# Differential attention scores from products of 64 rows in the two row halves of the TensorE array

## The chip, the cores and the metric

The kernel runs on one core of a Trainium2 chip. The metric is the device time in microseconds of one execution, as the median of several runs. Engines are named as in the profile: PE is the matrix engine (TensorE), PEld its weight loads, DVE the vector engine, ACT the scalar engine, POOL GpSimd, SP the queue that issues most DMAs.

## The reference

One layer of a streaming encoder on two inputs: a prompt of 1024 tokens (8 tiles of 128) and a running stream of 64 new tokens (the ninth tile, i = 8) with 128 cached keys and values. A norm and one input projection give two branches: retention (8 heads of 64) and differential attention (4 heads). Each differential head has two components of 64 columns with a softmax each, and values of 128 columns:

```
logits = einsum('bqhcd,bkhcd->bhcqk', q, k) * 64**-0.5      # c: two components
p = softmax(where(mask, logits, NEG_BIG))                   # block-causal, chunks of 64
w = p[:, :, 0] - lam * p[:, :, 1]
o = einsum('bhqk,bkhe->bqhe', w, v)
```

Both branches are normalised, gated and sent through an output projection; a residual add and a final norm close the layer. Everything is float32.

## The kernel before

The work is eight projection groups, alternately two retention heads (R, four times) and one differential head (D, four times). Group g makes, for each of 9 token tiles, a product `z` of the tile with 512 columns of the input weights, over 8 slices of the contraction; an output projection `zo` follows at the end. Projections and scores use fp32r, which keeps fewer bits; so each operand is split into a high part (rounded to fp32r) and a low part (what is left), and a projection is high·high + low·high + high·low.

After a projection, a chain of stages works on the tile: `diff_post` for D, `ret_post` for R. They are Python generators. Each `yield` gives a due time, in nanoseconds of PE work by the program's own count `clk.t`, and the buffers that the next stage needs. `pump`, called after each slice of a projection, issues the stages that are due and whose buffers are free. So the order on PE is fixed when the program is built, and PE works in that order: a late input stops everything behind it. The due times that matter here are D_QK and D_SPLIT (2600 each: from the projection to the transpose, from the transpose to the scores), D_SC (1600, between the two halves of the scores), D_SOFT and D_SOFT2 (3500 and 6500, from the scores to the transpose of the weights, for tiles with one and with two segments). `share` is new in the change; before, `mm` counts every product at its full columns.

A D tile goes like this, by the lines of the profile:
- L298 to L311: copy q and k, rotary on 16 columns.
- L323 (recorded at L68): two transposes into the PSUM tile `T`: 64 partitions of component 0, then 64 of component 1, for q and for k.
- L336 to L342, the split. Product operands of 128 rows are stacked: for component 0 `qs` is [high; low] of q, `khh` [high; high] of k and `kll` [low; low] of k, so that a product with `khh` and one with `kll` sum all four terms. It takes six ACT copies and six DVE differences on 64 partitions, alternating, component by component. `khh` and `kll` hold all keys of the head so far.
- L359 and L360 (recorded at L63): the scores `s`, per component and per segment of up to 512 keys, two products each. Tile i sees 128(i+1) keys: one segment up to i = 3, two from i = 4 to 7; tile 8 has one of 192. Each segment of a component has its own PSUM bank, tag `m`, of which there are five; transposes and the retention scores use the same tag.
- L363 (DVE): the negative maximum `nm`; L366 the smaller of two segments; L368 (ACT): the exponential `p` with its sum. These follow a component's products at once; component 1 comes a stage later.
- L376 to L381 (DVE): weights, p0 + factor·p1. L391 to L412: their transposes `wt` and the products `o` with v. L421: norm and gate, `mx`, transposed again as `mt`.

At tile 8 the cached keys come by DMA, already doubled to both halves, and are split by one ACT and one POOL instruction (L332, L333).

Of the kernel before, what the change touches and what calls it, by code (L numbers as in the profile page):

```python
# [20 lines left out]
SEQ = 1024  # L21
NS = 64
PAST = 128
# [3 lines left out]
NEG_BIG = -1e30  # L27
# [4 lines left out]
# PE time (ns) that the weave keeps between a stage of a tile's chain and the next one  # L32
D_QK, D_SPLIT, D_SC, D_SOFT, D_SOFT2, D_WT, D_WT2, D_NORM = 2600, 2600, 1600, 3500, 6500, 1600, 1300, 5000
# [6 lines left out]
WRAW, PB, QB = 3, 3, 3  # L40
SPACE, SPACE0 = 0, 4000
M_BUFS = 5
# [6 lines left out]
def body(ctx, tc, I, O):  # L49
    nc = tc.nc  # L50
    pe, act, dve, pool = nc.tensor, nc.scalar, nc.vector, nc.gpsimd
# [3 lines left out]
    class clk:  # L55
        t = 0.0

    def mm(out, lhsT, rhs, start, stop):
        n = 1
        for d in rhs.shape[1:]:  # L60
            n *= d
        clk.t += max(n, 256) / 2.37 if rhs.dtype == F32R else max(4 * n / 2.35, 214)
        pe.matmul(out, lhsT, rhs, start=start, stop=stop)  # L63
# [9 lines left out]
    sp = ctx.enter_context(tc.tile_pool(name="sp", bufs=2))  # L73
    ps = ctx.enter_context(tc.tile_pool(name="ps", bufs=2, space=PSUM))
# [33 lines left out]
    early = cp.tile([128, 424], F32, name="early")  # L108
# [15 lines left out]
    def rsq(out, ss, inv_n, n, rows):  # L124
        """out = (ss * inv_n + eps) ** -0.5"""
        dve.tensor_scalar(out, ss, inv_n, EPS, ALU.mult, ALU.add)  # L126
        pool.tensor_tensor(out, out, m05[:rows, :n], ALU.pow)  # L127
# [43 lines left out]
    # the first token tiles come together, one slice of d at a time  # L171
    for k in range(KD):
# [6 lines left out]
        hi = xh[:, 0:N0, k]  # L179
# [6 lines left out]
    late = cp.tile([128, 1656], F32, name="late")  # L186
# [24 lines left out]
    for b in range(2):  # L211
        t = cp.tile([128, 2, 128], F32, name=f"qpad{b}")
        pool.memset(t, 0.0)
        qpads.append(t)
        t = cp.tile([128, 256], F32, name=f"vpad{b}")
# [5 lines left out]
    state = {}  # L221
# [41 lines left out]
    KHH, KLL = {}, {}  # L263
# [14 lines left out]
    def diff_post(g, h, i):  # L278
        z = state.pop((g, i))
        rows = 128 if i < 8 else NS  # L280
        r = rstd[:rows, i:i + 1]
        nm = f"{g}_{i}"
        if i == 0:
            vbuf[h] = sp.tile([128, NT, 128], F32, tag="vb", name=f"v{h}", bufs=1)
            KHH[h] = sp.tile([128, 2, SEQ], F32R, tag="khh", name=f"khh{h}", bufs=1)
            KLL[h] = sp.tile([128, 2, SEQ], F32R, tag="kll", name=f"kll{h}", bufs=1)
# [4 lines left out]
        else:  # L291
            vs = sp.tile([NS, 128], F32, tag="vs", name=f"vs{h}", bufs=1)
            kd, vd = kbuf[h][:NS, 0], vs
            cv = sp.tile([128, 128], F32, tag="cv", name=f"cv{h}", bufs=1)
            nc.sync.dma_start(cv, I["cv"][h])
        qk = sp.tile([128, 4, 64], F32, tag="qk", name=f"qk{nm}", bufs=QB)
        q = qk[:rows]
# [3 lines left out]
        # partial rotary on the first 16 columns of each component  # L301
# [18 lines left out]
        # rows of T: 64 of component 0, then 64 of component 1  # L320
        T = ps.tile([128, 2, rows], F32, tag="m", name=f"T{nm}", bufs=M_BUFS)
        for c in range(2):
            tr(T[:, c, :], qk[:rows, 2 * c:2 * c + 2].rearrange("p a b -> p (a b)"))  # L323
        # component c of q as [hi; lo] (c = 0) and [lo; hi] (c = 1), of k as [hi; hi] and [lo; lo]
        qs = sp.tile([128, 2, 128], F32R, tag="qs", name=f"qs{nm}", bufs=1)
        qs = qs[:, :, :rows]
        khh, kll = KHH[h], KLL[h]
        o0, nk = (128 * i, 128 * (i + 1)) if i < 8 else (PAST, PAST + NS)
        if i == 8:
            ck = sp.tile([128, 2, PAST], F32, tag="rta", name=f"ck{h}", bufs=1)  # L330
            nc.sync.dma_start(ck, I["ck"][h])
            act.activation(khh[:, :, 0:PAST], ck, AF.Copy)  # L332
            pool.tensor_tensor(kll[:, :, 0:PAST], ck, khh[:, :, 0:PAST].bitcast(F32), ALU.subtract)  # L333
        for c in range(2):
            own, oth = slice(64 * c, 64 * c + 64), slice(64 - 64 * c, 128 - 64 * c)
            act.activation(qs[own, c], T[own, 0], AF.Copy, scale=0.125)  # L336
            dve.scalar_tensor_tensor(qs[oth, c], T[own, 0], 0.125, qs[own, c].bitcast(F32), ALU.mult, ALU.subtract)  # L337
            kc = khh[:, c, o0:o0 + rows]
            act.activation(kc[own], T[own, 1], AF.Copy)  # L339
            act.activation(kc[oth], T[own, 1], AF.Copy)  # L340
            for half in (own, oth):
                dve.tensor_tensor(kll[half, c, o0:o0 + rows], T[own, 1], kc[own].bitcast(F32), ALU.subtract)  # L342
# [4 lines left out]
        ns = len(segs)  # L347
# [3 lines left out]
        for c in range(2):  # L351
            p = sp.tile([128, 1024], F32, tag="p", name=f"p{nm}_{c}", bufs=PB)
            P.append(p)
            scs = []
            for n, bl in enumerate(segs):
                a, b = bl[0][0], bl[-1][0] + bl[-1][1]
                sc = ps.tile([128, 512], F32, tag="m", name=f"s{nm}_{c}_{n}", bufs=M_BUFS)
                scs.append((a, b, sc))
                mm(sc[:rows, 0:b - a], qs[:, c, :], khh[:, c, a:b], start=True, stop=False)  # L359
                mm(sc[:rows, 0:b - a], qs[:, c, :], kll[:, c, a:b], start=False, stop=True)  # L360
                if i < 8 and n == ns - 1:
                    dve.memset(sc[0:64, b - a - 64:b - a], NEG_BIG)  # L362
                dve.tensor_reduce(nm_[:rows, n, c:c + 1], sc[:rows, 0:b - a], AX.X, ALU.max, negate=True)  # L363
            mx_ = nm_[:rows, 0, c:c + 1]
            if ns == 2:
                dve.tensor_tensor(mx_, mx_, nm_[:rows, 1, c:c + 1], ALU.min)  # L366
            for n, (a, b, sc) in enumerate(scs):
                act.activation(p[:rows, a:b], sc[:rows, 0:b - a], AF.Exp, bias=mx_, accum_out=zz[:rows, n, c:c + 1])  # L368
            if c == 1:
                rel("qs")  # L370
            else:
                yield D_SC, {}
# [54 lines left out]
    def ret_post(g, p, i):  # L427
# [52 lines left out]
        # state update  # L480
# [28 lines left out]
    def rel(name):  # L509
        free[name] += 1  # L510
# [34 lines left out]
    def start_posts(force=False):  # L545
        """Begin the chains of the finished projections, oldest first."""
        while queue:
            g, kind, idx, i = queue[0]
            need = dict(gt=1) if kind == "D" else dict(gt=1, rv=1)
            now = force or g > 0  # L550
            if not now and clk.t < posted[0] + SPACE0:
                return
            if not grab(need):
                if not now:
                    return
                pump(True)
# [43 lines left out]
    def outproj(n, i):  # L600
# [5 lines left out]
        # the last tile goes in two halves, so that less follows its last product  # L606
# [89 lines left out]
def _consts():  # L696
# [3 lines left out]
    def tab(dim, theta):  # L700
# [20 lines left out]
            xs=(64, 1024), early=(128, 424), late=(128, 1656), ck=(4, 128, 2, 128), cv=(4, 128, 128), st=(4, 128, 128),  # L721
# [5 lines left out]
def _layout(a):  # L727
# [17 lines left out]
    ck = a["cache_k"][0, 0].reshape(PAST, 4, 2, 64).transpose(1, 3, 2, 0)  # L745
    d["ck"] = np.concatenate([ck, ck], 1)
# [43 lines left out]
```

## Time and the profile before

| | |
|---|---|
| median of 3 runs | 722.19 us (722.11 to 723.34) |
| profiled execution, first to last instruction | 719.0 us |
| mean granted clock of PE | 0.989 |
| PE busy | 677.6 us, 94% |
| DVE busy | 484.1 us, 67% |
| ACT busy | 364.7 us, 51% |
| POOL busy | 201.7 us, 28% |

The profiled execution's time is known only as its span, first to last instruction; the median of the runs, which also holds what lies around the span, is 3.2 us more. Durations of PE rows overlap, since products are pipelined; the distance from one start to the next is the time that one takes. In rows of the timeline the first figure is the start in us from the span's start, the second the duration; the two shapes of a PE row, as in 64\*128 64x128, are rows and columns of the array in use, and rows and columns of the moving operand. What stands in square brackets is idle time of the engine before the row and what ended it.

### The profile page before, as it was taken

Reading aid. Unit: us, or ns where it says so; the run is one execution under the profiler, and the core shown is the slowest. Engines: PE = TensorE matmul, PEld = TensorE weight load, DVE = VectorE, ACT = ScalarE, POOL = GpSimd, SP = SyncE. Lnnn points to the kernel's source line nnn. Section 1 sums busy time; section 2 is a strip of 40 time slices with the busy share of each in tenths; the row PEclk is TensorE's granted clock in tenths of the full one; section 3 lists DMA queues with packets and bytes.
Section 4 is the critical chain, followed back from the end, with each engine's and each line's share of the span. In section 5 each row is a group of like instructions: output and inputs, shape, how many; then the busy total and the mean of one; then the engine's idle time right before and its main releaser. Section 6 shows DMA issues by size and latency. Waiting matters only on the chain.

```text
span 719.0 us, 10737 instructions
## 1 busy us (share of the span) xinstructions
PE 677.6 (94%) x3360; PEld 541.1 (75%) x3360; DVE 484.1 (67%) x1451; ACT 364.7 (51%) x1258; POOL 201.7 (28%) x316
## 2 busy tenths in 40 slices
PE   8899898989999999999999999899999998999996
PEld 5687677867787778767887787678877785778885
DVE  5478857878566678795566788866587788742322
ACT  4575645666335455763344556733266567632322
POOL 4443511132223311322225111422251114032332
PEclk9999999999999999999999999999999999999999
DMA  7872400032001300140004000310051003342442
GB/s 237 284 258 64 133 26 17 16 95 78 14 8 58 94 23 8 47 135 13 9 8 143 10 23 37 100 55 10 8 162 51 15 1 102 107 142 73 139 146 112
DMA packets 35129, 55.04 MB, mean 77 GB/s; under 512 B 6080, under 2 KB 20160, under 8 KB 35072
## 3 DMA queue, kind: packets, MB, share of 16 engines
q1 hardware_dynamic: 34784, 53.88, 23.2%
q8 instruction: 26, 0.43, 0.2%
q10 hardware_dynamic: 288, 0.48, 0.2%
q14 instruction: 31, 0.25, 0.1%
HBM read 41.01 MB, written 13.34 MB: 76 GB/s over the span
## 4 chain that ended last, share of the span: by engine, by line
PE 55%; DVE 25%; ACT 8%; DMA 5%; issue 4%; POOL 3%; SPq 0%; POOLq 0%; ACTq 0%; DVEq 0%
PE z L63 31%; PE zo L63 11%; PE o L63 5%; PE s L63 5%; DVE nm L363 4%; DVE kll L342 3%; ACT p L368 3%; DVE p L381 3%; POOL ss L127 2%; PE T L68 1%; DVE qs L337 1%; DMA x<-in_x 1%; DMA xraw<-in_xtp 1%; DVE rz L377 1%; DVE rta L448 1%
## 5 line engine op out<-in xcount | busy, mean ns | idle before, releaser
L63 PE MATMUL z<-ws,xh 128*128 128x512 f32 x1152 | 406.4, 412 | 2.9 <-DVE gt L257 1.9
L63 PEld LDWEIGHTS z<-ws,xh 128*128 128x128 f32 x1152 | 217.2, 191 | 46.7 <-DVE gt L257 2.3
L63 PE MATMUL z<-ws,xl 128*128 128x512 f32 x512 | 202.7, 396 | 2.4 <-DVE xl L181 2.4
L63 PEld LDWEIGHTS z<-ws,xl 128*128 128x128 f32 x512 | 98.2, 192 | 16.3 <-DVE xl L181 3.2
L63 PE MATMUL zo<-ws,xh 128*128 128x512 f32 (+1 forms) x304 | 89.8, 381 | 0.0
L127 POOL TENSOR_TENSOR ss<-ss,m 128x2 f32<-128x2 f32 (+2 forms) x72 | 46.4, 644 | 143.2 <-DVE ss L126 135.4
L368 ACT ACTIVATE p<-s,nm 128x384 f32<-128x384 f32 (+4 forms) x104 | 58.4, 564 | 38.6 <-DVE nm L363 20.7
L63 PEld LDWEIGHTS zo<-ws,xh 128*128 128x128 f32 x304 | 56.2, 188 | 10.9 <-issue 0.2
L96 POOL TENSOR_TENSOR ws<-wr,ws 128x512 fp32r<-128x512 f32 x36 | 52.3, 1463 | 29.5 <-ACT ws L91 29.5
L363 DVE TENSOR_REDUCE nm<-s 128x1 f32<-128x384 f32 (+4 forms) x104 | 55.6, 537 | 2.5 <-PE s L63 0.8
L91 ACT ACTIVATE ws<-wr 128x512 fp32r<-128x512 f32 x80 | 47.5, 626 | 14.3 <-DMA wr<-in_wo 8.9
L306 POOL TENSOR_TENSOR ta<-qk,early 128x64 f32<-128x64 f32 (+1 forms) x36 | 11.7, 324 | 150.2 <-ACT qk L298 150.1
L63 PE MATMUL zo<-ws,xl 128*128 128x512 f32 (+1 forms) x136 | 51.3, 377 | 0.0
L63 PEld LDWEIGHTS o<-v,wT 128*128 128x128 f32 x288 | 38.7, 194 | 16.3 <-DVE mx L421 5.5
L342 DVE TENSOR_TENSOR kll<-T,khh 64x128 fp32r<-64x128 f32 (+1 forms) x144 | 40.4, 280 | 13.4 <-ACT khh L340 10.6
L445 POOL TENSOR_TENSOR rta<-rqk,late 128x256 f32<-128x256 f32 (+1 forms) x36 | 28.6, 794 | 73.5 <-DVE rqk L437 73.4
L63 PE MATMUL o<-v,wT 128*128 128x128 f32 x288 | 42.6, 285 | 5.7 <-DVE mx L421 3.1
L272 ACT ACTIVATE mix<-mt 128x128 f32<-128x128 f32 (+1 forms) x72 | 19.5, 271 | 50.7 <-PE mt L68 50.5
L63 PE MATMUL s<-khh,qs 128*128 128x384 f32 (+4 forms) x104 | 39.9, 384 | 3.1 <-DVE s L362 1.2
L339 ACT ACTIVATE khh<-T 64x128 fp32r<-64x128 f32 (+1 forms) x72 | 19.0, 264 | 37.1 <-DVE qs L337 36.5
L63 PE MATMUL s<-kll,qs 128*128 128x384 f32 (+4 forms) x104 | 36.1, 350 | 1.8 <-DVE kll L342 1.1
L96 DVE TENSOR_TENSOR ws<-wr,ws 128x512 fp32r<-128x512 f32 x44 | 29.3, 685 | 11.5 <-ACT ws L91 11.4
(143 smaller groups left out, 1076.5 us busy)
## 6 DMA issues: line engine op xcount, KB each, us to landing
wr<-in_wg SPq DMA_DIRECT2D x28, 512.0 KB, 4.6
xk<-in_xp SPq DMA_DIRECT2D x8, 512.0 KB, 5.4
wr<-in_wo SPq DMA_DIRECT2D x8, 512.0 KB, 4.3
xr<-in_xp SPq DMA_DIRECT2D x16, 256.0 KB, 2.6
mixd<-mix SPq DMA_DIRECT2D x28, 128.0 KB, 1.7
x<-in_x SPq DMA_DIRECT2D x8, 256.0 KB, 4.1
wr<-in_wg SPq DMA_DIRECT2D x8, 256.0 KB, 4.9
xraw<-in_xtp SPq DMA_DIRECT2D x8, 256.0 KB, 4.3
```

What stands on the lines that cost most here:

```text
L63: pe.matmul(out, lhsT, rhs, start=start, stop=stop)
L91: act.activation(s[:, 0, :], raw_w[g, k // 2][:, k % 2, :], AF.Copy)
L96: eng.tensor_tensor(s[:, 1, :], raw_w[g, k // 2][:, k % 2, :], s[:, 0, :].bitcast(F32), ALU.subtract)
L127: pool.tensor_tensor(out, out, m05[:rows, :n], ALU.pow)
L272: act.activation(mixbuf[g, c][:, off:off + rows], tp[:, :rows], AF.Copy)
L306: pool.tensor_tensor(ta[:rows, 0], src, C, ALU.mult)
L339: act.activation(kc[own], T[own, 1], AF.Copy)
L342: dve.tensor_tensor(kll[half, c, o0:o0 + rows], T[own, 1], kc[own].bitcast(F32), ALU.subtract)
L363: dve.tensor_reduce(nm_[:rows, n, c:c + 1], sc[:rows, 0:b - a], AX.X, ALU.max, negate=True)
L368: act.activation(p[:rows, a:b], sc[:rows, 0:b - a], AF.Exp, bias=mx_, accum_out=zz[:rows, n, c:c + 1])
L381: dve.scalar_tensor_tensor(wt[:rows, a:b], P[1][:rows, a:b], rz[:rows, 2:3], P[0][:rows, a:b], ALU.mult, ALU.add)
L445: pool.tensor_tensor(ta[:rows, 0].rearrange("p a (b d) -> p (a b) d", b=2), q.rearrange("p a (b d) -> p (a b) d", b=2), C, ALU.mult)
```

## The change

The stacked copies go. `qh`, `ql`, `kh`, `kl` keep both components as they come out of the transpose, component 0 in partitions 0 to 63 and component 1 in 64 to 127. The split is two ACT and two DVE instructions of 128 partitions. Scores are three terms (high·high, low·high, high·low), each a product of 64 rows, for component 0 in the lower row half of the array and for component 1 in the upper, alternately, into two banks. The segment is now the outer loop and the component the inner one, with a stage (D_SC) between segments; the exponentials follow after all segments. `mm` counts such a product at half its time (`share=2`). The cached keys are loaded once, not doubled. Some comments are dropped.

```
-    def mm(out, lhsT, rhs, start, stop):
+    def mm(out, lhsT, rhs, start, stop, share=1):
...
+        clk.t += (max(n, 256) / 2.37 if rhs.dtype == F32R else max(4 * n / 2.35, 214)) / share
...
-            KHH[h] = sp.tile([128, 2, SEQ], F32R, tag="khh", name=f"khh{h}", bufs=1)
-            KLL[h] = sp.tile([128, 2, SEQ], F32R, tag="kll", name=f"kll{h}", bufs=1)
+            KH[h] = sp.tile([128, SEQ], F32R, tag="khh", name=f"kh{h}", bufs=1)
+            KL[h] = sp.tile([128, SEQ], F32R, tag="kll", name=f"kl{h}", bufs=1)
...
-            ck = sp.tile([128, 2, PAST], F32, tag="rta", name=f"ck{h}", bufs=1)
+            ck = sp.tile([128, PAST], F32, tag="rta", name=f"ck{h}", bufs=1)
             nc.sync.dma_start(ck, I["ck"][h])
-            act.activation(khh[:, :, 0:PAST], ck, AF.Copy)
-            pool.tensor_tensor(kll[:, :, 0:PAST], ck, khh[:, :, 0:PAST].bitcast(F32), ALU.subtract)
-        for c in range(2):
-            own, oth = slice(64 * c, 64 * c + 64), slice(64 - 64 * c, 128 - 64 * c)
-            act.activation(qs[own, c], T[own, 0], AF.Copy, scale=0.125)
-            dve.scalar_tensor_tensor(qs[oth, c], T[own, 0], 0.125, qs[own, c].bitcast(F32), ALU.mult, ALU.subtract)
-            kc = khh[:, c, o0:o0 + rows]
-            act.activation(kc[own], T[own, 1], AF.Copy)
-            act.activation(kc[oth], T[own, 1], AF.Copy)
-            for half in (own, oth):
-                dve.tensor_tensor(kll[half, c, o0:o0 + rows], T[own, 1], kc[own].bitcast(F32), ALU.subtract)
+            act.activation(kh[:, 0:PAST], ck, AF.Copy)
+            pool.tensor_tensor(kl[:, 0:PAST], ck, kh[:, 0:PAST].bitcast(F32), ALU.subtract)
+        act.activation(qh, T[:, 0], AF.Copy, scale=0.125)
+        dve.scalar_tensor_tensor(ql, T[:, 0], 0.125, qh.bitcast(F32), ALU.mult, ALU.subtract)
+        kc = kh[:, o0:o0 + rows]
+        act.activation(kc, T[:, 1], AF.Copy)
+        dve.tensor_tensor(kl[:, o0:o0 + rows], T[:, 1], kc.bitcast(F32), ALU.subtract)
         yield D_SPLIT, dict(p=2)
...
         for c in range(2):
-            p = sp.tile([128, 1024], F32, tag="p", name=f"p{nm}_{c}", bufs=PB)
-            P.append(p)
-            scs = []
-            for n, bl in enumerate(segs):
-                a, b = bl[0][0], bl[-1][0] + bl[-1][1]
-                sc = ps.tile([128, 512], F32, tag="m", name=f"s{nm}_{c}_{n}", bufs=M_BUFS)
-                scs.append((a, b, sc))
-                mm(sc[:rows, 0:b - a], qs[:, c, :], khh[:, c, a:b], start=True, stop=False)
-                mm(sc[:rows, 0:b - a], qs[:, c, :], kll[:, c, a:b], start=False, stop=True)
+            P.append(sp.tile([128, 1024], F32, tag="p", name=f"p{nm}_{c}", bufs=PB))
+        scs = []
+        for n, bl in enumerate(segs):
+            if n > 0:
+                yield D_SC, {}
+            a, b = bl[0][0], bl[-1][0] + bl[-1][1]
+            sc = [ps.tile([128, 512], F32, tag="m", name=f"s{nm}_{c}_{n}", bufs=M_BUFS) for c in range(2)]
+            scs.append((a, b, sc))
+
+            terms = [(qh, kh), (ql, kh), (qh, kl)]
+            for t, (ql_, kl_) in enumerate(terms):
+                for c in range(2):
+                    half = slice(64 * c, 64 * c + 64)
+                    mm(sc[c][:rows, 0:b - a], ql_[half], kl_[half, a:b], start=(t == 0), stop=(t == 2), share=2)
+            for c in range(2):
                 if i < 8 and n == ns - 1:
-                    dve.memset(sc[0:64, b - a - 64:b - a], NEG_BIG)
-                dve.tensor_reduce(nm_[:rows, n, c:c + 1], sc[:rows, 0:b - a], AX.X, ALU.max, negate=True)
-            mx_ = nm_[:rows, 0, c:c + 1]
-            if ns == 2:
-                dve.tensor_tensor(mx_, mx_, nm_[:rows, 1, c:c + 1], ALU.min)
+                    dve.memset(sc[c][0:64, b - a - 64:b - a], NEG_BIG)
+                dve.tensor_reduce(nm_[:rows, n, c:c + 1], sc[c][:rows, 0:b - a], AX.X, ALU.max, negate=True)
+        rel("qs")
+        if ns == 2:
+            dve.tensor_tensor(nm_[:rows, 0], nm_[:rows, 0], nm_[:rows, 1], ALU.min)
+        for c in range(2):
             for n, (a, b, sc) in enumerate(scs):
-                act.activation(p[:rows, a:b], sc[:rows, 0:b - a], AF.Exp, bias=mx_, accum_out=zz[:rows, n, c:c + 1])
-            if c == 1:
-                rel("qs")
-            else:
-                yield D_SC, {}
+                act.activation(P[c][:rows, a:b], sc[c][:rows, 0:b - a], AF.Exp, bias=nm_[:rows, 0, c:c + 1],
+                               accum_out=zz[:rows, n, c:c + 1])
...
-    ck = a["cache_k"][0, 0].reshape(PAST, 4, 2, 64).transpose(1, 3, 2, 0)
-    d["ck"] = np.concatenate([ck, ck], 1)
+    d["ck"] = a["cache_k"][0, 0].transpose(1, 2, 0)
```

More of the change, by code (lines that the diff above doesn't have):

```diff
@@ L61, in mm @@
             n *= d
-        clk.t += max(n, 256) / 2.37 if rhs.dtype == F32R else max(4 * n / 2.35, 214)
+        clk.t += (max(n, 256) / 2.37 if rhs.dtype == F32R else max(4 * n / 2.35, 214)) / share
         pe.matmul(out, lhsT, rhs, start=start, stop=stop)
@@ L262, in body @@
     kbuf, vbuf = {}, {}
-    KHH, KLL = {}, {}
+    KH, KL = {}, {}
     def mix_out(g, i, mx, rows):
@@ L325, in diff_post @@
         qs = sp.tile([128, 2, 128], F32R, tag="qs", name=f"qs{nm}", bufs=1)
-        qs = qs[:, :, :rows]
-        khh, kll = KHH[h], KLL[h]
+        qh, ql = qs[:, 0, :rows], qs[:, 1, :rows]
+        kh, kl = KH[h], KL[h]
         o0, nk = (128 * i, 128 * (i + 1)) if i < 8 else (PAST, PAST + NS)
         if i == 8:
-            ck = sp.tile([128, 2, PAST], F32, tag="rta", name=f"ck{h}", bufs=1)
+            ck = sp.tile([128, PAST], F32, tag="rta", name=f"ck{h}", bufs=1)
             nc.sync.dma_start(ck, I["ck"][h])
-            act.activation(khh[:, :, 0:PAST], ck, AF.Copy)
-            pool.tensor_tensor(kll[:, :, 0:PAST], ck, khh[:, :, 0:PAST].bitcast(F32), ALU.subtract)
-        for c in range(2):
-            own, oth = slice(64 * c, 64 * c + 64), slice(64 - 64 * c, 128 - 64 * c)
-            act.activation(qs[own, c], T[own, 0], AF.Copy, scale=0.125)
-            dve.scalar_tensor_tensor(qs[oth, c], T[own, 0], 0.125, qs[own, c].bitcast(F32), ALU.mult, ALU.subtract)
-            kc = khh[:, c, o0:o0 + rows]
-            act.activation(kc[own], T[own, 1], AF.Copy)
-            act.activation(kc[oth], T[own, 1], AF.Copy)
-            for half in (own, oth):
-                dve.tensor_tensor(kll[half, c, o0:o0 + rows], T[own, 1], kc[own].bitcast(F32), ALU.subtract)
+            act.activation(kh[:, 0:PAST], ck, AF.Copy)
[5 more added lines that the diff above has]
+        dve.tensor_tensor(kl[:, o0:o0 + rows], T[:, 1], kc.bitcast(F32), ALU.subtract)
         yield D_SPLIT, dict(p=2)
@@ L720 @@
 _INS = dict(wg=(8, 128, 8, 512), wo=(2, 128, 8, 512), x0=(128, 8, N0, 128), xtp=(8 - N0, 128, 8, 128), xts=(128, 8, 64), xp=(1024, 1024),
-            xs=(64, 1024), early=(128, 424), late=(128, 1656), ck=(4, 128, 2, 128), cv=(4, 128, 128), st=(4, 128, 128),
+            xs=(64, 1024), early=(128, 424), late=(128, 1656), ck=(4, 128, 128), cv=(4, 128, 128), st=(4, 128, 128),
             lamv=(128, 4, 64), fng=(128, 1024))
```

## The prediction

> **What bounds the kernel now.** I read the head of the page first (busy time by engine, the chain that ended last), then the instructions of the score tile `s`, then the timeline of the TensorE rows and of its weight loads around the scores.
>
> ```profile
> span 719.0 us, 10737 instructions
> PE 677.6 (94%) x3360; PEld 541.1 (75%) x3360; DVE 484.1 (67%) x1451; ACT 364.7 (51%) x1258; POOL 201.7 (28%) x316
> PE 55%; DVE 25%; ACT 8%; DMA 5%; issue 4%; POOL 3%; SPq 0%; POOLq 0%; ACTq 0%; DVEq 0%
> PE z L63 31%; PE zo L63 11%; PE o L63 5%; PE s L63 5%; DVE nm L363 4%; DVE kll L342 3%; ACT p L368 3%; DVE p L381 3%; POOL ss L127 2%; PE T L68 1%; DVE qs L337 1%; DMA x<-in_x 1%; DMA xraw<-in_xtp 1%; DVE rz L377 1%; DVE rta L448 1%
> ```
>
> TensorE (PE) is busy 94% of the span and holds 55% of the chain, most of it projections (`z`, `zo`) that the change leaves alone. DVE holds 25%, and the lines that the change touches are in it: `nm` (maximum of the scores), `kll` and `qs` (the splits of k and q). So the change is worth two things: PE time of the score products, and waits of PE for the splits.
>
> The profiled execution spans 719.0 us; the median of the runs is 722.19, 3.2 more. I sum against 719.0 and add 3.2.
>
> **The products.** These rows are their number and their pace where nothing is late:
>
> ```profile
> L63 PE MATMUL s<-khh,qs x104: 221/397/618, 101.8 to 622.2; 128*128 128x384 f32 x40, 128*128 128x512 f32 x32, 128*128 128x256 f32 x16, 128*128 128x128 f32 x8
> 442.43 0.39 PE L63 MATMUL s<-kll,qs 128*128 128x512 f32 x1
> 442.65 0.34 PE L63 MATMUL s<-khh,qs 128*128 128x384 f32 x1
> 442.82 0.34 PE L63 MATMUL s<-kll,qs 128*128 128x384 f32 x1
> 443.00 0.39 PE L63 MATMUL z<-ws,xh 128*128 128x512 f32 x1
> 706.89 0.28 PE L63 MATMUL zo<-ws,xl 128*128 128x256 f32 x1
> 707.01 0.40 PE L63 MATMUL zo<-ws,xh 128*128 128x256 f32 x2
> 163.44 0.97 PEld L63 LDWEIGHTS o<-v,wT 128*128 128x128 f32 x8 [0.34 <-DVE mx L421]
> ```
>
> The durations overlap, so the step from start to start is the price: about 0.23 us for 512 columns (0.22 here), 0.175 for 384, 0.12 for 256. Eight weight loads of 128 columns in a row end after 0.97 with the last one 0.19 long, a step of 0.11; that is the floor of every product. The 104 `khh` products are two components of 52 segments: 16 segments of 512 columns, 20 of 384, 8 of 256, and 8 of 128 or 192, which I price at the floor. Now a segment has 4 products: 0.92, 0.70, 0.48, 0.44 us, over all segments 14.7+14.0+3.8+3.5 = 36.0 us. After the change it has 6 products of 64 rows, three pairs whose members lie in different row halves and write different banks. No row shows such a pair, so I bound it.
> - Both halves fully at once: three steps instead of four, −9.1 us.
> - One after the other: six instead of four, +18.2 us.
> - Together, but with weight loads one at a time: a pair then takes the longer of one product and two loads (0.22), and the second half trails by 0.11. A segment costs 0.80, 0.725, 0.67, 0.66, against now −0.12×16 +0.025×20 +0.19×8 +0.22×8 = **+1.9 us**.
>
> I take the last: rows show a load running under another instruction's product everywhere, and never two loads at once. So even in the good case the products give nothing; six loads eat what three pairs would save.
>
> **Entering and leaving 64 rows.** The trace of before has products of 64 rows, in retention tile 8:
>
> ```profile
> 245.60 0.40 PE L63 MATMUL z<-ws,xh 128*128 128x512 f32 x1
> 245.92 0.43 PE L63 MATMUL s<-qpad,rkT 128*64 128x128 f32 x2
> 246.29 0.49 PE L63 MATMUL s<-vpad,rqk 64*128 64x128 f32 x2
> 246.70 0.50 PE L63 MATMUL z<-ws,xh 128*128 128x512 f32 x1
> 247.04 0.39 PE L63 MATMUL z<-ws,xl 128*128 128x512 f32 x1
> 245.92 0.19 PEld L63 LDWEIGHTS s<-qpad,rkT 128*64 128x64 f32 x2 [0.37 <-issue]
> 246.28 0.29 PEld L63 LDWEIGHTS s<-vpad,rqk 64*128 64x128 f32 x2 [0.17 <-issue]
> 246.70 0.19 PEld L63 LDWEIGHTS z<-ws,xh 128*128 128x128 f32 x1
> 321.47 0.14 PEld L63 LDWEIGHTS s<-khh,qs 128*64 128x64 f32 x1
> ```
>
> Usually a weight load starts under the product before it. Here the loads at 245.92, 246.28 and 246.70 start only after the product before has left the array, "issue" ended two of the gaps (nothing was waited for), and the product must then wait for its load. From 245.60 to 247.04 are 1.44 us; the work in it is two projections of 0.23 and four passes at 0.11, 0.90. The other 0.54 are three changes of the array's shape (128 by 128, to 64 columns, to 64 rows, back): **0.18 us each**. The new scores enter 64 rows and leave it once per segment: 104 changes, 18.7 us. The low end is 0: the load at 321.47, of today's scores of tile 8 (fp32r, 64 columns), has no gap ahead of it, so fp32r with fewer columns pays nothing; none with fewer rows is in the trace. I take 18.7, because two different row halves can't be addressed without splitting the rows, while fewer columns can simply leave columns unused. Where PE waits before a segment anyway, the entry is hidden; I allow 3 us of the 18.7 for that (16 or 17 of the 52).
>
> The Trainium skill has a rule on this: "TensorEngine Tiling (Array Packing)", Key Properties, says that changing the tiling mode, not just the tile, drains TensorE. The trace agrees at 0.18 us a change for fp32; no run here shows it for fp32r rows. By that rule the sum is the one below; without it 15.7 less, which is the first rival.
>
> **The splits.** Per tile, 6 ACT and 6 DVE instructions of 64 partitions become 2 and 2 of 128:
>
> ```profile
> L342 DVE TENSOR_TENSOR kll<-T,khh 64x128 fp32r<-64x128 f32 (+1 forms) x144 | 40.4, 280 | 13.4 <-ACT khh L340 10.6
> L337 DVE SCALAR_TENSOR_TENSOR qs<-T,qs 64x128 fp32r<-64x128 f32 (+1 forms) x72 | 20.2, 281 | 14.2 <-ACT qs L336 12.1
> L340 ACT ACTIVATE khh<-T 64x128 fp32r<-64x128 f32 (+1 forms) x72 | 19.1, 265 | 0.9
> L339 ACT ACTIVATE khh<-T 64x128 fp32r<-64x128 f32 (+1 forms) x72 | 19.0, 264 | 37.1 <-DVE qs L337 36.5
> L336 ACT ACTIVATE qs<-T 64x128 fp32r<-64x128 f32 (+1 forms) x72 | 18.9, 263 | 31.0 <-DVE kll L342 26.2 <-PE T L68 4.5
> L485 DVE TENSOR_TENSOR S<-S,s 128x128 f32<-128x128 f32 x32 | 9.1, 285 | 11.5 <-PE o L63 11.3
> L458 ACT ACTIVATE rkT<-T 128x128 f32<-128x128 f32 (+1 forms) x36 | 9.7, 270 | 31.8 <-PE T L68 31.8
> L63 PEld LDWEIGHTS s<-khh,qs 128*128 128x128 f32 (+1 forms) x104 | 19.3, 186 | 9.0 <-ACT khh L340 3.1 <-ACT v L299 2.9 <-DVE qs L337 1.7
> L63 PEld LDWEIGHTS s<-kll,qs 128*128 128x128 f32 (+1 forms) x104 | 19.4, 187 | 6.8 <-DVE kll L342 5.5 <-issue 0.2
> 406.50 0.38 PE L68 MATMUL T<-ident,qk 128*128 128x128 f32 x2
> 410.04 0.44 PE L63 MATMUL s<-khh,qs 128*128 128x384 f32 x1 [0.19 <-ACT khh L340]
> 410.66 0.45 PE L63 MATMUL s<-kll,qs 128*128 128x384 f32 x1 [0.18 <-DVE kll L342]
> 410.95 0.39 PE L63 MATMUL z<-ws,xh 128*128 128x512 f32 x1
> ```
>
> Full partitions cost the same as half (285 against 280 ns, 270 against 265). DVE loses 60.6 − 72×0.285 = 40.1 us, ACT 57.0 − 72×0.27 = 37.6; both lie beside PE and aren't in the sum themselves. What is in it is lateness. In the last rows q and k are transposed at 406.50, and 3.5 us later the first product still waits for `khh`, the second for `kll`; the two take 0.91 where two of 384 take 0.35. The chain of 12 that alternates between two engines becomes one of 4, with 8 instructions, some 2.2 us, less work. In sum the score loads show 9.0+6.8 = 15.8 us of idle time, of which part is hidden under a product (and 2.9 is for another wait, `v`). Bounds of the gain are 4 and 13; I take **−9**. What is late next is DVE's queue: `ql` and `kl` still stand behind whatever DVE has before them.
>
> **The softmax and the banks.** Scores now come by segment, both components together. With two segments (16 of 36 tiles) the exponentials of component 0 can't start until both second segments are reduced: after the last product come two reductions, the minimum and four exponentials, where it was two.
>
> ```profile
> L368 ACT ACTIVATE p<-s,nm 128x384 f32<-128x384 f32 (+4 forms) x104 | 58.4, 564 | 38.6 <-DVE nm L363 20.7 <-DVE nm L366 17.0
> L68 PE MATMUL wt<-ident,p 128*128 128x128 f32 (+2 forms) x152 | 25.5, 275 | 7.0 <-DVE p L381 7.0
> ```
>
> Two more at 0.56 put the weights `p` 1.1 us later against an unchanged due time (D_SOFT2), and PE already waits 7.0 us for `p`. Ends: 0, and 16×1.1 = 18 if nothing covers it. I take **+2**, near zero, as the same tile's split is over 2 us shorter and the single-segment tiles lose a stage (D_SC). The four score banks of a tile, of five under tag `m`, are also held some 1 to 2 us longer; I put that at nothing while the next user of a bank is five allocations away, and price it as a rival. The weave takes a product at half time (share=2), so the later stages come due a little later in real time: this only adds slack. The cached k is loaded half as large (4 DMAs, at tile 8): the POOL and ACT instructions on it halve, off the path, priced 0.
>
> **Sum.** 719.0 + 1.9 (products) + 18.7 − 3 (changes) − 9 (splits) + 2 (softmax) = 729.6; plus 3.2: **733 us**, 1.5% slower. With each term between its likely ends (changes 10 to 19, products −9 to +2, splits −5 to −13, softmax 0 to 5) this case lies between 722 and 741.
>
> **Rivals.**
> 1. Fp32r pays no change of shape, and the halves run together. For it: the load at 321.47. Against: the rows at 246. The 15.7 fall away and the products cost between −9.1 and +1.9: 719 − 7 − 9.1 (or + 1.9) + 3.2 = 706 to 717, say **712**. This is the one that ends faster; it decides once the 104 changes together cost under 8.1 us (18.7 less the 10.6 that the forecast lies above 722.2), 0.08 each.
> 2. The halves run one after the other, with the changes: 719 + 18.2 + 15.7 − 7 + 3.2 = 749.1, **749**. For it: no row shows two products at once, and the two 64-row ones at 246.29 do run in turn (the same half, though). Against: their operands, array rows and banks are disjoint.
> 3. Neither: no shape change and no overlap, so the change doesn't do what it says: 719 + 18.2 − 7 + 3.2 = **733**, the forecast's time with another trace.
> 4. The banks: PE stands in order behind an `m` tile whose bank still waits for exponentials, up to 4×0.56 = 2.2 us in some of the 16 tiles; at half of that, 18 us over the forecast: **751**.
>
> 5. The changes are paid, but loads and products of the two halves all run at once: three steps a segment, 719 − 9.1 + 15.7 − 7 + 3.2 = **722**, no change. For it: the halves share no array row. Against: the rows show loads one at a time.
>
> The Trainium skill's page "TensorE: Matmul & The Clock Gate", Part 3, says that tiles in different row groups run concurrently, loads under products too, and gives 3.07 times for four tiles of 32 rows at 512 columns. No row here shows it; it speaks for rival 5 and against 2 and 3.
>
> **Chances.** Forecast 0.42, rival 1 0.15, rival 2 0.18, rival 3 0.08, rival 4 0.05, rival 5 0.12. A change within 0.2% (720.7 to 723.6) can't be told from none in this kernel. Faster: nearly all of rival 1, a tenth of the forecast and a third of rival 5, 0.23; same, from the last two: 0.05; slower 0.72. The range 716 to 752 leaves out most of rival 1 and the top of rivals 2 and 4, about 0.2.
>
> **What the profile after would show.** Changes: the load of the first score product of a segment, and of the first product after it, starts after the product before has ended, with "issue" as releaser; in rival 1 and 3 it starts under it. Pairs: the starts of two score products of a segment lie under 0.11 apart, three pairs of 512 in about 0.8 us; in rival 2 six steps of 0.23. Splits: DVE busy about 40 us less, ACT 38, the score loads' idle time for `kh` and `kl` well under 15.8. Softmax and banks: PE's idle time for `p` (7.0 now) grows, or score products wait for ACT's exponentials. I am wrong if a change costs nothing in fp32r, if the loads of two halves run at once, or if the shorter split chain frees more than the score waits, since DVE has 25% of the chain.

## The result: slower by 33.8 us, and the profile after

The kernel after takes 755.9 us in the median of 4 runs (753.5 to 756.2), the kernel before 722.15 in 4 runs on the same chip: a ratio of 1.0468 (95% interval 1.0451 to 1.0485). The forecast was 733, in a range of 716 to 752. Its direction is right; the size lies outside.

The head of the page after, and the first lines of its chain of work:

```profile
span 754.1 us, 10629 instructions
PE 695.9 (92%) x3464; PEld 543.6 (72%) x3464; DVE 433.7 (58%) x1291; ACT 325.5 (43%) x1114; POOL 201.7 (27%) x316
PE 69%; DVE 14%; ACT 5%; DMA 5%; POOL 4%; issue 3%; SPq 0%; POOLq 0%; DVEq 0%; ACTq 0%
```

DVE lost 50.4 us of work, 40 of it in the rows of the split, and ACT 39.2, and DVE's share of the chain fell from 25% to 14%. What was lightened did get lighter, and the kernel got slower. PE's own work has 18.3 us more busy time, so the next view is the granted clock (before, then after), and the one after it PE's waits.

```profile
core 0: 719.0 us, clock 0.989
core 0: 754.1 us, clock 0.966
```

A span at clock c lacks about (1−c) of itself: 7.9 us before, 25.6 after.

PE's waits (engine and tile that waits, engine, tile and line it waits for: us in all, times, longest), the largest rows that concern the change, first before, then after:

```profile
PE wt L68 <- DVE p L381: 7.0, 5, 2.1
PE o L63 <- DVE at L469: 4.3, 6, 0.9
PE o L63 <- DVE mx L421: 3.9, 5, 0.8
PE o L63 <- DVE wT L398: 2.6, 3, 1.5
```

```profile
PE o L63 <- DVE mx L421: 11.9, 6, 2.6
PE o L63 <- ACT wT L400: 8.3, 5, 3.0
PE wt L68 <- DVE p L381: 6.8, 10, 1.6
PE wt L68 <- ACT p L371: 5.2, 3, 1.8
PE o L63 <- DVE at L469: 4.1, 5, 0.9
```

All rows of this view together come to 33.9 us before and 51.2 after. With that the result divides (us; the last column is span less waits less lost clock):

| kernel | span | clock | PE's waits | lost to the clock | rest |
|---|---|---|---|---|---|
| before | 719.0 | 0.989 | 33.9 | 7.9 | 677.2 |
| after | 754.1 | 0.966 | 51.2 | 25.6 | 677.3 |

So the work of PE itself, with the new products and their changes of shape in it, takes what it took before. The 35 us are about 17 of waits and 16 to 18 of clock. The division is approximate, since the mean clock also counts half clock while PE waited or was done. With only the half clock under working PE counted from the trace's clock records, the loss is 6.8 us before and 22.8 after; the rest, without the last 6 or 7 us in which PE has nothing left to do, is then 672 and 674 us, and 668 to 674 in every other run below except e12 (697). So apart from e12 the kernels differ in waits and clock, hardly in work.

The waits are not the old ones: those of the score products for the splits (2.9 us before, in three rows) are gone from the list, and those that grew belong to later stages, the product with v (`o`) and the transposes of the weights (`wt`).

Where such a wait arises, in the timeline of after (start, duration, instruction; in brackets idle time before it and what ended it); it is the end of the first head, where tile 8 follows tile 7:

```profile
190.22 0.40 PE L63 MATMUL z<-ws,xh 128*128 128x512 f32 x1
190.46 1.05 PE L63 MATMUL o<-v,wT 128*128 128x128 f32 x8
...
191.63 0.37 ACT L417 ACTIVATE junk<-o,rz 128x128 f32<-128x128 f32 x1 [0.79 <-PE o L63]
...
192.36 0.54 POOL L127 TENSOR_TENSOR ss<-ss,m 128x1 f32<-128x1 f32 x1 [10.15 <-DVE ss L126]
...
193.21 0.35 DVE L421 SCALAR_TENSOR_TENSOR mx<-o,ss,gt 128x128 f32<-128x128 f32 x1 [0.93 <-POOL ss L419]
193.61 0.43 PE L63 MATMUL o<-cv,wT 128*64 128x128 f32 x2 [2.10 <-DVE mx L421]
...
197.03 0.63 PE L63 MATMUL z<-ws,xl 128*128 128x512 f32 x1
197.45 1.00 PE L63 MATMUL z<-ws,xh 128*128 128x512 f32 x2
```

Tile 7's products `o` end at 191.5; a norm then goes through ACT, POOL and DVE, and `mx` has read the bank at 193.56. Tile 8's `o`, which needs that same bank (there is one), is the next thing in PE's order: 2.10 us idle. The last two rows show what follows: a projection of 512 columns takes 0.42 from start to start instead of 0.23. The stretch in the windows view (length; busy us of PE, PEld, DVE, ACT, POOL with counts; granted clock; DMA share; GB/s):

```profile
193.00:199.00 6.00, 5.39 (x19) 4.18 (x20) 3.42 (x10) 1.08 (x4) 1.62 (x4) 0.72 0.05 14
```

A clock of 0.72 over 6 us is 3.4 us at half speed. This wait of 2 us so cost another 1.7. The same place recurs at each of the four heads, with waits of 2.1 to 2.6 us, 9.4 in all. Before, three of the four had no wait there and one had 0.78; in the first head 2.4 us of other work stood between the two (three dots stand for it):

```profile
180.29 1.16 PE L63 MATMUL o<-v,wT 128*128 128x128 f32 x8
...
183.87 0.43 PE L63 MATMUL o<-cv,wT 128*64 128x128 f32 x2
```

### The profile page after: what moved, and what is told of

The parts are those of the page before. It is cut to its first block, busy times and chain, and to the rows that moved or that the text cites. A ratio compares the mean times of both kernels' runs of the same rounds, so it can differ in the third digit from the quotient of the medians.

```text
span 754.1 us, 10629 instructions
## 1 busy us (share of the span) xinstructions
PE 695.9 (92%) x3464; PEld 543.6 (72%) x3464; DVE 433.7 (58%) x1291; ACT 325.5 (43%) x1114; POOL 201.7 (27%) x316
## 4 chain that ended last, share of the span: by engine, by line
PE 69%; DVE 14%; ACT 5%; DMA 5%; POOL 4%; issue 3%; SPq 0%; POOLq 0%; DVEq 0%; ACTq 0%
PE z L63 40%; PE zo L63 12%; PE s L63 7%; PE o L63 6%; DMA x<-in_x 3%; PE wt L68 2%; DVE p L381 2%; ACT p L371 2%; PE T L68 2%; POOL ss L127 2%; DVE nm L365 1%; DVE rta L448 1%; DVE ws L96 1%; POOL ws L96 1%; PE mt L68 1%
## 5 line engine op out<-in xcount | busy, mean ns | idle before, releaser
L63 PE MATMUL z<-ws,xh 128*128 128x512 f32 x1152 | 414.4, 421 | 1.9 <-DVE gt L257 1.9
L63 PEld LDWEIGHTS z<-ws,xh 128*128 128x128 f32 x1152 | 220.6, 194 | 58.5 <-issue 9.4
L63 PE MATMUL z<-ws,xl 128*128 128x512 f32 x512 | 204.9, 400 | 3.5 <-DVE xl L181 3.5
L96 POOL TENSOR_TENSOR ws<-wr,ws 128x512 fp32r<-128x512 f32 x36 | 51.2, 1438 | 41.6 <-ACT ws L91 41.3
L365 DVE TENSOR_REDUCE nm<-s 128x1 f32<-128x384 f32 (+4 forms) x104 | 52.1, 535 | 4.4 <-PE s L63 4.2
L63 PE MATMUL o<-v,wT 128*128 128x128 f32 x288 | 43.7, 290 | 11.4 <-ACT wT L400 8.3
L68 PE MATMUL wt<-ident,p 128*128 128x128 f32 (+2 forms) x152 | 26.7, 287 | 16.8 <-DVE p L381 6.8
L68 PEld LDWEIGHTS wt<-ident,p 128*128 128x128 f32 (+2 forms) x152 | 18.3, 144 | 27.3 <-DVE p L381 8.3
L448 DVE TENSOR_TENSOR rta<-rqk,late 128x128 f32<-128x128 f32 (+1 forms) x72 | 35.2, 518 | 0.9
L298 ACT ACTIVATE qk<-z,rstd 128x256 f32<-128x256 f32 x32 | 15.2, 475 | 46.7 <-PE z L63 46.6
```

What stands on the lines that cost most here:

```text
L68: pe.transpose(out, in_, ident[:n, :n])
L96: eng.tensor_tensor(s[:, 1, :], raw_w[g, k // 2][:, k % 2, :], s[:, 0, :].bitcast(F32), ALU.subtract)
L298: act.activation(q, z[:rows, 0:256].rearrange("p (c d) -> p c d", c=4), AF.Copy, scale=r)
L365: dve.tensor_reduce(nm_[:rows, n, c:c + 1], sc[c][:rows, 0:b - a], AX.X, ALU.max, negate=True)
L448: dve.tensor_tensor(ta[:rows, 1, :, 32 * half:32 * half + 32], q[:, :, 32 - 32 * half:64 - 32 * half], rcs[:rows, i, 1 + half].unsqueeze(1 ...
```

## The experiments

The texts put down ahead of the runs, which call the issuing of the stages the weave, name three theories. A is the order: both components' exponentials start late in the new order of stages, the program issues the later stages before their inputs are there, and the waits bring half clock. B is the array: the products of 64 rows and their changes of shape disturb PE wherever they stand. C, from e3 on, is the count: the program counts the new products at half. The first four runs are meant to pull these apart; from e5 on A stands for the order in which the weave issues the stages, B for the late exponentials of two-segment tiles alone.

**e1_due: later due times.**

```
-D_QK, D_SPLIT, D_SC, D_SOFT, D_SOFT2, D_WT, D_WT2, D_NORM = 2600, 2600, 1600, 3500, 6500, 1600, 1300, 5000
+D_QK, D_SPLIT, D_SC, D_SOFT, D_SOFT2, D_WT, D_WT2, D_NORM = 2600, 2600, 1600, 5500, 9500, 1600, 1300, 5000
```

> The changed kernel with later due times after the scores only: D_SOFT 3500 to 5500, D_SOFT2 6500 to 9500. Theory A (order): the score block itself is no dearer than before; the loss comes after it, since both components' exponentials now start late, the weave issues the transposes of the weights and the products with v before their data is there, PE waits in order, and the long waits halve its clock. Then later due times take back most of the loss: 720 to 735 us, PE clock back to 0.98 or more, PE's idle time for p, wT and mx together under 20 us. Theory B (array): the 64-row products, by their changes of shape, disturb PE and its clock wherever they stand; due times change little: 750 to 758, clock about 0.966.

Measured: 774.5 us, 1.0728 (1.0691 to 1.0765). It went the other way: waits 63 us, clock 0.940, and the wait of `o` for `mx` went from 11.9 to 21.8 us. Neither theory had that: later due times alone do not bring the loss back, they add to it. A reading of the code, not measured: the three places of the gate tile `gt` fill up when chains last longer, and the program then issues stages ahead of their due time all the same.

**e2_order: before's stacked operands, splits and products, in the change's order and stages.** Against the kernel after, the products read (its splits and operands, not shown, are those of before):

```
-            for t, (ql_, kl_) in enumerate([(qh, kh), (ql, kh), (qh, kl)]):
-                for c in range(2):
-                    ...  mm(..., ql_[half], kl_[half, a:b], ..., share=2)
+            for c in range(2):
+                mm(sc[c][:rows, 0:b - a], qs[:, c, :], khh[:, c, a:b], start=True, stop=False)
+                mm(sc[c][:rows, 0:b - a], qs[:, c, :], kll[:, c, a:b], start=False, stop=True)
```

> The kernel before, with stacked operands and its 128-row products and 12 split instructions, but with the new order alone: segment outer, both components together, D_SC between segments only, all exponentials after the last segment, due times as they are. Theory A: the loss is in the order, so this is slow too, 740 to 765 us (it keeps the waits for the splits that the change removed), with a clock under 0.975. Theory B: the order is nearly free, 720 to 726, clock about 0.99.

Measured: 814.8 us, 1.1297 (1.1257 to 1.1337), clock 0.947. Its PE waits:

```profile
PE s L63 <- DVE qs L337: 23.5, 12, 2.9
PE o L63 <- DVE mx L423: 19.6, 8, 2.8
PE wt L68 <- DVE p L383: 19.0, 12, 3.2
```

There is no product of 64 rows in this kernel's scores, and it is slower still, more than A allowed. So the order does harm without them, and the new products and splits take back 59 us. The first row is the split, now late for both components at once; with `khh` and `kll` it comes to 37.7 us of waits that the kernel after does not have. The other two are the rows that grew in the kernel after.

**e3_share1: the new products counted at their full columns.** `share=2` is left out.

> The changed kernel with its score products counted in full in the weave's clock (share=1), nothing else. A third theory, C (count): halving the count makes the weave believe that less PE time has passed than has. Counting in full brings later stages earlier in the order of PE. If A holds, that gives the softmax less cover: the same or slower, 755 to 765. If the halved count were the harm (C), 725 to 740. By B no change, 753 to 758.

Measured: 738.7 us, 1.0215 (1.0161 to 1.027), 17 us less than after. That is where C had it, and it looks like proof that the count is the cause; e9 below says otherwise.

**e4_firstmax: exponentials straight behind each segment's maxima**, with the first segment's maximum as the shift for both (the second is still computed, unused).

```
-        rel("qs")
-        if ns == 2:
-            dve.tensor_tensor(nm_[:rows, 0], nm_[:rows, 0], nm_[:rows, 1], ALU.min)
-        for c in range(2):
-            for n, (a, b, sc) in enumerate(scs):
+            for c in range(2):
                 act.activation(P[c][:rows, a:b], ...)
+        rel("qs")
```

> The changed kernel, with each segment's exponentials issued right after that segment's maxima, and the first segment's maximum as the shift for both segments (a softmax does not depend on the shift; the second segment's maxima are still computed, but not used). It takes away only the wait of the first segment's exponentials for the second segment, and with it the burst of four exponentials and the longer hold of the first segment's two banks. Theory A with the two-segment tiles as its cause: 720 to 738, PE's idle time for exponentials (banks), p and wT together falls from 20 us to under 10. If only the due times of the one-segment tiles matter: 745 or more. Theory B: 750 to 758.

Measured: 742.4 us, 1.0285 (1.0261 to 1.0309), 13.5 less than after, between the two ranges that A gave it. The late exponentials of the two-segment tiles are worth something, though not the whole.

**e5_weave, e6_weave_first, e7_unpaired: towards the best order.** e5 counts the products at 1/1.5 and gives tiles with one segment back the stage that the change took from them. e6 is e5 with e4's edit. e7 is e6 with the three products of component 0 issued ahead of the three of component 1.

```
+++ e5
-                    mm(..., share=2)
+                    mm(..., share=1.5)
...
+        if ns == 1:
+            yield D_SC, {}
+++ e7
-            for t, (ql_, kl_) in enumerate(terms):
-                for c in range(2):
+            for c in range(2):
+                for t, (ql_, kl_) in enumerate(terms):
```

> The changed kernel with the weave's timing of before put back and nothing else: score products count two thirds (share=1.5, so that six half-row products count what four full ones did), and one-segment tiles get their D_SC stage back, behind the scores. The order of PE's stages, and the stages that are forced ahead of their due time, are then nearly those of before. In the trace of the changed kernel the score groups themselves, changes of shape and all, take 44.3 us of PE against 48.4 before. Theory A (the order of the weave does the harm, the 64-row products none): 715 to 730 us, clock 0.98 or more, PE's waits as in the kernel before, those of the two-segment softmax a little longer. Theory B (the late joint exponentials of two-segment tiles do it, whatever the weave's order): 735 to 745, as in the run with the early exponentials, which took 13 us back. Theory C (the halved count alone): 735 to 742, as with share=1.

> The same, with each segment's exponentials right behind its maxima and the first segment's maximum as the shift of both (second maxima computed, not used). Theory A: 712 to 725, up to 8 us below the run without it. Theory B: this edit carries most of the gain: 715 to 725, 15 us or more below the run without it.

> The same as the run before it in this call, but the three products of component 0 come first and then those of component 1, so that only one pair of neighbours per segment lies in different row halves. Pairing theory: two products of different row halves run at once (starts 3 ns apart in the trace of the changed kernel), so taking the pairing away costs about two product steps per segment, 16x0.46+20x0.35+8x0.24+8x0.22 = 18 us: 12 to 20 us slower than its pair. If the halves gained nothing: the same within 3 us.

Measured: e5 725.3 us, 1.0036 (1.001 to 1.0062). e6 722.1, 1.0007 (0.9988 to 1.0027). e7 **715.3, 0.9905 (0.9884 to 0.9927)**, the fastest kernel of the case with e11, 1% under the kernel before. What was expected of e7, that its halves would run in turn, did not come. Its timeline:

```profile
288.23 0.62 PE L63 MATMUL s<-kh,qs 64*128 64x384 f32 x4
288.68 0.34 PE L63 MATMUL s<-kl,qs 64*128 64x384 f32 x2
288.96 0.50 PE L63 MATMUL z<-ws,xh 128*128 128x512 f32 x1
```

The six products are over when three steps are, as in the kernel after: component 1's, issued behind all three of component 0, started 10 ns behind their counterparts (single starts in the trace; the rows put them together as x4 and x2). So this order of issue does not matter to the halves, and the 6.8 us between e6 and e7 are not the array's, nor of PE's waits (29.9 and 30.3): up to PE's last product e6 has 23.9 us at half clock and e7 13.7, which is 5.1 us of the difference. What sets off the one and not the other is open.

**e8_before_first: e4's edit alone, in the kernel before.** Exponentials use the first segment's maximum.

> Control: the kernel before with each segment's exponentials right behind its maxima and the first segment's maximum as the shift. Tells how much of the early exponentials' gain has nothing to do with the change. Theory A and B: little to gain where components follow one another, 715 to 723. If the softmax bounds the kernel before too: under 712.

Measured: 723.3 us, 1.0021 (1.0002 to 1.0039). By itself the edit is worth nothing, so e7's lead is not this edit's alone.

**e9_count and e10_stage: e5's two edits, each alone.** e9 has `share=1.5`; e10 has the stage and leaves `share=2`:

```
+++ e10
+        if ns == 1:
+            yield D_SC, {}
         rz = ...
```

> The changed kernel with share=1.5 alone (the score products count as much as before), the one-segment tiles still without their D_SC stage. Both edits together took 30 us back, share=1 alone took 17. If the count does the harm: 725 to 735. If the missing stage does: 745 to 756. Either way the span should be PE's waits, plus half of the time at half clock, plus 676 us within 3.

> The changed kernel with the D_SC stage put back behind the scores of one-segment tiles alone, share=2 as it is. If the missing stage does the harm: 725 to 735. If the count does: 745 to 756. If each does its part: both runs between 730 and 748. The same sum as in the other run.

Measured: e9 759.5 us, 1.0506 (1.0486 to 1.0526); e10 **723.7, 1.0015 (0.9998 to 1.0031)**. e9 is slower than either of its theories had it; e10 is where the missing stage was to put it, or a little better. In both, the span is the sum that the text gives, within 3 us. Two added lines take back 32.2 us of the 33.8. The half count is not the cause: at 1.5, which counts the scores as before, it is no better than at 2. That e3 helped because at full count the order happens to shift elsewhere is an argument, not shown. PE's waits of e10:

```profile
PE o L63 <- ACT wT L402: 7.1, 5, 2.0
PE wt L68 <- ACT p L371: 6.9, 4, 1.8
PE o L63 <- DVE at L471: 3.8, 5, 0.9
PE o L63 <- DVE mx L423: 0.9, 3, 0.4
```

The wait for `mx` went from 11.9 to 0.9 us; all waits come to 33.4, the clock to 0.987, the span to 721.7: both parts of the loss are gone. Of nine waits over 1.5 us in e10 two were followed by half clock, in the kernel after 11 of 15. The same place in its timeline, tile 7's and tile 8's `o`:

```profile
177.29 1.16 PE L63 MATMUL o<-v,wT 128*128 128x128 f32 x8
178.38 0.33 PE L68 MATMUL wt<-ident,p 64*128 64x64 f32 x2
178.64 0.70 PE L63 MATMUL s<-qpad,rkT 128*128 128x256 f32 x2
...
180.55 0.39 PE L63 MATMUL z<-ws,xh 128*128 128x512 f32 x1
180.88 0.43 PE L63 MATMUL o<-cv,wT 128*64 128x128 f32 x2
```

Between the end of the first `o` (178.45) and the start of the second (180.88) now stand 2.4 us of other work, and no row here has a wait, nor have the other three heads at this place: the spacing of the kernel before is back. Tile 8 has one segment; without the stage its chain came 1.6 us of PE work (by the program's count) earlier and ran into the back of tile 7's, which has two. This place holds 9.4 us of the waits that e10 took away, and three stretches of half clock behind it another 5.1: some 14.5 of the 32 us. The rest is spread over other places and not followed one by one.

Whether it is the 1.6 us or the place in the order is not separated. By the code, `pump` issues a stage only when its number is below that of the chain ahead, so a chain with one stage less stands a step closer to the one ahead, whatever its due time. e1 gave one-segment tiles 2.0 us more and did not help, but it also gave the others 3.0.

**e11_merged: e7 with both segments in one go**, so that 16 tiles change the shape twice less (36 groups of products instead of 52).

```
-        for n, (a, b, sc) in enumerate(scs):
-            if n > 0:
-                yield D_SC, {}
...
+        rel("qs")
+        yield D_SC, {}
```

> The fastest run so far (weave of before, early exponentials, component by component), with both segments of a two-segment tile in one go: 36 groups of 64-row products instead of 52, so 32 changes of the array's shape less, at about 0.15 us each from the score groups of the changed kernel. Price theory: 708 to 712, 3 to 7 us below it. Rival, banks: four of the five score banks must be free at once, PE waits for them: 716 or more.

Measured: 715.2 us, 0.990 (0.9879 to 0.992), the same as e7. That lies between what the price of the changes and the rival of the banks would give. Where nothing was late the groups did get shorter: 1.51 us for six products of 512 and six of 384, where two groups of e7 took 0.99 and 0.82. The gain did not reach the time: the waits come to 31.1 us against 30.3, with 4.0 for `kh` new and 11.0 for `mx` (9.1 in e7), and the clock is 0.986 against 0.988.

**e12_onehalf: e7 with the products of both components on the lower half of the rows** (component 1 is left out; component 0 is computed twice).

```
-                    half = slice(64 * c, 64 * c + 64)
+                    half = slice(0, 64)
```

> The fastest run so far with the products of component 1 taken from the lower row half too (it leaves out component 1: its scores are computed from component 0's rows). Everything else stands as it is. All six products of a segment then need the same rows. Taking the component order apart in the earlier run did not take the pairing away: the trace shows the halves running side by side there too, 10 ns apart. Pairing theory: here they run in turn, starts a whole product apart, 0.69 us more per segment of 512, 0.52 of 384, 0.36 of 256, 0.33 of the rest: score groups 27 us longer, 735 to 748 us. If the array runs one product after another anyway and the short starts are an effect of the records: the same within 3 us.

Measured: 736.0 us, 1.0184 (1.0164 to 1.0205), 20.7 us more than e7. Its timeline, a segment of 384 as in e7's above:

```profile
295.32 0.62 PE L63 MATMUL s<-kh,qs 64*128 64x384 f32 x2
295.78 0.34 PE L63 MATMUL s<-kl,qs 64*128 64x384 f32 x1
295.96 0.52 PE L63 MATMUL s<-kh,qs 64*128 64x384 f32 x2
296.32 0.34 PE L63 MATMUL s<-kl,qs 64*128 64x384 f32 x1
296.59 0.50 PE L63 MATMUL z<-ws,xh 128*128 128x512 f32 x1
```

From the first score product to the projection behind it 1.27 us, in e7 0.73. Over all 52 groups, from the end of the step before them to the start after them, this is 69.2 us against 43.7. So two halves do share the time, and that is worth 25.5 us in the groups and 20.7 in the whole, since e12 has 23.3 us of waits where e7 has 30.3.

## Why the prediction was wrong in size

That the forecast named the right direction is luck. The terms that were to make the kernel slower, products and changes, come to nothing together with the splits (the rest of 677 us in both kernels), and nearly all that made it slower comes from the step put at +2. One sum does not come out either: the ends named for the terms add up to 710 to 743 us, not 722 to 741.

**The softmax and the banks, +2: this step failed.** The sentence that fails says that "the single-segment tiles lose a stage (D_SC)" and counts it as cover for the rest. A stage is not only a delay of one tile: it holds that tile's chain apart from its neighbour's in a fixed order with one bank for `o`. Its loss is worth +32 us (e10), 17.8 of waits and 14 to 16 of clock by the trace, against the +2 that stands for the whole step. The mechanism I priced, later exponentials in 16 tiles against an unchanged due time, is there (`wt` waits for `p` of DVE and ACT 12.0 us in after, 7.0 before), but e10 still has 8.6 of it and can't be told from before. "This only adds slack" of the half count is not shown either way: 1.5 instead of 2 made 3.6 us of difference, upwards, within the shifts of order.

What the trace of before could have told: the row of `o` waiting for `mx`, 3.9 us in 5 waits, none over 0.8. One of them, 0.78, lies where tile 8 follows tile 7. It was a near miss already, with the stage in.

**The clock was left out of the sum.** No term had one, since the granted clock of before was 0.989. The price of a PE wait of 2 us can then be 2 us plus 1.7. That is about half of the missing time.

**The products, +1.9: mis-sized.** I took weight loads one at a time. The rows of after, a segment of 384, matmuls and then weight loads:

```profile
432.28 0.27 PE L68 MATMUL mt<-ident,mx 128*128 128x128 f32 x1
432.48 0.62 PE L63 MATMUL s<-kh,qs 64*128 64x384 f32 x4
432.94 0.34 PE L63 MATMUL s<-kl,qs 64*128 64x384 f32 x2
433.21 0.50 PE L63 MATMUL z<-ws,xh 128*128 128x512 f32 x1
433.55 0.40 PE L63 MATMUL z<-ws,xl 128*128 128x512 f32 x1
...
432.48 0.30 PEld L63 LDWEIGHTS s<-kh,qs 64*128 64x128 f32 x4 [0.29 <-ACT junk L417]
432.77 0.19 PEld L63 LDWEIGHTS s<-kl,qs 64*128 64x128 f32 x2
433.21 0.19 PEld L63 LDWEIGHTS z<-ws,xh 128*128 128x128 f32 x1 [0.25 <-PE s L63]
```

Four loads end 0.30 after the first start, where four at 0.11 with the last one 0.19 long would need 0.52; the two halves' loads run together, as their products do (a pair starts 3 ns apart). So a segment is three steps, the −9.1 of rival 5. The Trainium skill's "TensorE: Matmul & The Clock Gate", Part 3, says that row groups run concurrently; this case's runs agree, for two groups and fp32r, by e12's 20.7 us.

**The changes of shape, +18.7 − 3: right.** They are paid in fp32r too. In the fence above the load of `z` starts only after the scores, 0.25 idle, and the next projection follows 0.34 behind the first instead of 0.23. The whole kernel's weight loads show it, the first two rows before and the last two after:

```profile
PEld s L63 <- issue: 1.9, 8, 0.4
PEld z L63 <- issue: 1.0, 6, 0.2
PEld z L63 <- issue: 9.4, 33, 0.6
PEld s L63 <- issue: 7.7, 30, 0.4
```

A segment, with the late load of the projection behind it, takes three steps and about 0.40 more (1.10 us for 512, 0.92 for 384, 0.75 for 256), so 0.20 a change against 0.18. The Trainium skill's "TensorEngine Tiling (Array Packing)", Key Properties, has that drain; the trace agrees, at these 0.20 us. With the three steps this is 36.0 − 9.1 + 104 × 0.20 = 47.7 us for the products where they ideally took 36.0.

**The splits, −9: right, a little small.** No row of PE's waits of after has a score product waiting for `qs` or `kl`. Before, the score groups took 48.4 us from the end of the step ahead of them to the next start, 12.4 over their ideal 36.0; by the loads' releasers in the prediction's rows most of that is late splits. After, it is 44.3. With the late load of the projection behind the group counted in (up to one step before the second start behind it) it is 49.1 before and 50.6 after, of which the 47.7 are products and changes: what the halves and the splits gained, the changes of shape took, as the table's rest of 677 in both kernels has it.

**The rivals.** Rival 5 gave 722 for changes paid and halves fully at once. That is the change without its lost stage: e10, 723.7. Rival 1 is out by the gaps, 2 and 3 by e12 and the timeline. Rival 4 had a true picture, PE in order behind a bank that is not free, and the wrong bank: `o`, not `m`. Its 751 lies near the result by luck.

**Open.** Why later due times cost more (e1), why full count (e3) and early exponentials (e4) each take back part of the loss without the stage, why e6 has more half clock than e7, and whether a lost stage harms by its time or by its place. All are shifts of one fixed order, and no run holds everything but one wait equal.

## What to carry to other kernels

When an edit merges, drops or moves a stage of a hand-woven order, price that before the arithmetic: list the single buffers that neighbouring chains share, read how near each wait on them already is, and ask which chain now runs into the one ahead. Ask it of the shortest chain, that of the last tile, first. Allow, for each new TensorE wait near 2 us, for a stretch at half clock behind it, and keep the number of stages the same in a first trial of new arithmetic, so that the two can be told apart.

## What the hardware showed that I had not expected

- A wait of about 2 us can be enough for the clock to halve. In the traces' clock records half clock came in stretches of 3.41 us, or several of them, and in each of the 14 traces any two of them start a whole number of 3.41 us apart: as far as these traces show, they keep a beat of their own, and a wait can only make one of its steps slow. The waits ahead were mostly 1.6 to 3.2 us long, as in the rows at 193.61, but not each such wait did it: one of 2.31 us that ended at 85.4 in the kernel before had no half clock behind it, one of 2.32 us that ended at 85.2 in the kernel after had. Up to PE's last product the stretches sum to 13.7 us before and 47.8 after. The Trainium skill's "TensorE: Matmul & The Clock Gate", in the section on HAM oscillation, has idle gaps of over some 3.4 us for this; here shorter ones did it, and the measurement decides.
- The two row halves take work from one instruction order as if each had an order of its own: in e7, component 1's first product ran 10 ns behind component 0's although two more of component 0 were issued ahead of it.
- Weight loads of two row halves run at the same time, four in 0.30 us.
